# Expert results scaled by their places' weights and added to one DRAM array by accumulating scatters, in a four-layer mixer and expert kernel

## The chip, the cores and the metric

The kernel runs on one core of one Trainium2 chip. The metric is the device time in microseconds of one execution, the median of several runs. Engines are named as in the profile: PE (TensorE, with its weight loads PEld), DVE (VectorE), ACT (ScalarE), POOL (GpSimd), SP (SyncE, which here only issues transfers). "P" is 128 partitions.

## The reference

One sequence of 512 tokens with 1024 features goes through two blocks of two layers each. The first block (latent attention, retention, gated linear attention, two feed-forward networks with a convolution) is not touched. Each layer of the second block is a mixer, a layer norm, and then 16 experts in four groups, of which every token uses two:

```python
def hier_moe(x, ...):
    t = x.reshape(B * S, D)                                   # 512 x 1024
    g_prob = softmax(t @ w_group + b_group)
    g_val, g_idx = lax.top_k(g_prob, 1)
    e_logits = (einsum('td,gde->tge', t, w_expert) + b_expert)[chosen group]
    e_val, e_idx = lax.top_k(softmax(e_logits), 2)
    weights = g_val * e_val / sum(e_val)
    combine = ...                                             # 512 x 16, two entries a token
    hid = silu(t @ w_gate[e]) * (t @ w_up[e])                 # for each of 16 experts
    out = sum over e of combine[:, e] * (hid @ w_down[e])
...
ffn = hier_moe(h, ...)
h = layer_norm(DN_ALPHA * h + ffn, ln_g, ln_b)
```

## The kernel before

The kernel is one instruction stream for each engine, written in a tile framework that tracks which instruction reads and writes which tile, sets the semaphores, and puts each engine's instructions in an order of its own by priority (the order of the program) and readiness; on an engine, and on a DMA queue, they then run strictly in that order. "If" blocks are closed units: nothing moves across them.

Layers 2 and 3 (tags m0 and m1) end in the part that is changed. It has four steps:

1. `out_proj_ln` finishes the layer's first norm, one tile of 128 tokens after the other (`hN[t]`, two halves of 512 features); `store` writes each to a DRAM array `dx`. `router` computes logits on PE beside it.
2. `choose` picks two experts a token. From a running count it gives each token a `rank`, its place in the list of its expert (128 places in an expert). `places` turns this round: `eq` is a one-hot matrix of places, and 16 small matmuls give `idx`, the token of each place. `rows_of_y` computes for each token the two rows of `dy` where its results will stand, and its two weights.
3. `experts` loops over 16 experts. The weights of an expert are three transfers of 1 MB from SP into four raw buffers; each is split into a rounded half (`whi`, ACT, line 146) and a rest (`wlo`, DVE, or POOL for the third, line 147) so that three fast matmuls give one exact one. `fetch` gathers an expert's token rows from `dx` (POOL, line 1854, three buffers `X`), PE transposes them (line 1868), two products, a gate and a third product follow (lines 160 to 163), and the result `Y` (two buffers, 128 x 1024) is copied out of PSUM by ACT and DVE (lines 188 and 190) and written as a plain 512 KB transfer to `dy` (`put`, line 1859, on SP's queue among the weights). After the loop an "If" holds further rounds for experts with more than 128 tokens; it is passed over when there are none.
4. `combine` gathers for each token tile two sets of rows from `dy` (eight gathers on POOL, line 1831), scales one or both by ACT (line 1999), adds them on DVE or POOL (lines 2001 to 2006) and norms the sum (`layer_norm`, lines 1478 to 1502). After layer 2 the normed tiles go to the first projections of layer 3 (transposes at line 2057); after layer 3 they are stored as the output (line 2253).

In `combine` four of the eight gathers land in the ring of raw weight buffers (`wraw`), so that layer 3's first weights wait for them.

Of the kernel before, what the change touches and what calls it, by code (L numbers as in the profile page):

```python
# [26 lines left out]
class Ctx:  # L27
    def __init__(self, tc, ctx):
# [1631 lines left out]
NE = 16  # L1660
BIG = 1.0e30
# [11 lines left out]
def router(K, hN, A, D, tag):  # L1673

    nc, c, small = K.nc, K.const, K.small
    V, G = nc.vector, nc.gpsimd
    AD, MU, SU = ALU.add, ALU.mult, ALU.subtract
    w0, b0, gc, bcol, io, pcol, tokb, eb = (K.load(A[n]) for n in (tag + "_wr", tag + "_br", tag + "_gc", tag + "_bc", "iota", "pcol", "tokb", "eb"))  # L1680
    keep = lambda n, shape, dt=F32: K.gconst.tile(shape, dt, name=tag + n)
# [45 lines left out]
    R = dict(rank=keep("rank", [P, 8]), rhs=keep("rhs", [P, 8, 2, 16], BF16), idx=keep("idx", [P, 16], I32), row=keep("row", [P, 8], I32), eb=keep("eb", [P, 8]),  # L1727
             w=keep("w", [P, 2, 4, 1]), wr=keep("wr", [P, 8]), more=keep("more", [P, 1], I32), io=io,
             al=keep("al", [P, 1]))
    V.memset(R["al"], ALPHA)  # L1730
    rank, rhs, w12 = R["rank"], R["rhs"], R["w"]

# [9 lines left out]
    def choose():  # L1742
# [29 lines left out]
        places(K, R, K.sm(), eq_tile(K))  # L1772
# [11 lines left out]
        V.tensor_tensor(out=w12[:, 0], in0=gv, in1=m, op=MU)  # L1784
        V.tensor_tensor(out=w12[:, 1], in0=w12[:, 0], in1=r, op=MU)
# [19 lines left out]
def places(K, R, ps, eq):  # L1805
# [7 lines left out]
    V.tensor_scalar(out=R["idx"], in0=ps[:, 0:16], scalar1=OOB, scalar2=None, op0=ALU.add)  # L1813


def rows_of_y(K, R):

    V, AD, MU = K.nc.vector, ALU.add, ALU.mult
    m, f = (K.small.tile([P, 8], F32, tag=n, name=n, bufs=1) for n in ("rym", "ryf"))
    V.tensor_scalar(out=m, in0=R["rank"], scalar1=0.0, scalar2=None, op0=ALU.is_ge)  # L1820
# [4 lines left out]
    V.tensor_scalar(out=R["row"], in0=f, scalar1=OOB, scalar2=None, op0=AD)
    V.tensor_tensor(out=R["wr"], in0=R["w"].rearrange("p k t o -> p (k t o)"), in1=m, op=MU)


def gather(K, D, R, i, Y):

    K.nc.gpsimd.indirect_dma_start(out=Y, out_offset=None, in_=D["y"], in_offset=bass.IndirectOffsetOnAxis(ap=R["row"][:, i:i + 1], axis=0),  # L1831
                                   bounds_check=NE * P - 1, oob_is_err=False)


def experts(K, hN, A, D, R, rows, tag):
# [22 lines left out]
    def put(e, Y):  # L1858
        nc.sync.dma_start(D["y"][e * P:(e + 1) * P], Y)
# [72 lines left out]
    def more(e):  # L1932
# [18 lines left out]
        for i in range(2):  # L1951
# [3 lines left out]
            V.tensor_copy(out=X[:, cs], in_=ps)  # L1955
# [3 lines left out]
    with ExitStack() as ifs:  # L1959
        for rd in range(1, NR):  # L1960
            ifs.enter_context(tc.If(n > rd - 1))
            if rd == 1:
                for o in hN:
                    for x in o:
                        V.tensor_scalar(out=x, in0=x, scalar1=ALPHA, scalar2=None, op0=ALU.mult)
                V.memset(R["al"], 1.0)
            for i in range(8):
                gather(K, D, R, i, Xs[0])
                for b in range(2):
                    o = hN[i % 4][b]  # L1970
                    V.scalar_tensor_tensor(out=o, in0=Xs[0][:, b * 512:b * 512 + 512], scalar=R["wr"][:, i:i + 1], in1=o,
                                           op0=ALU.mult, op1=ALU.add)
            V.tensor_scalar(out=R["rank"], in0=R["rank"], scalar1=-float(CAP), scalar2=None, op0=ALU.add)
            rows_of_y(K, R)
            places(K, R, sm, eq)
            for e in range(NE):
                more(e)
    return Xs, gb


def combine(K, hN, D, R, Xs, gb):


    nc, V = K.nc, K.nc.vector
    AD, MU = ALU.add, ALU.mult
    Ys = Xs + [K.small.tile([P, 1024], F32, tag="Y", name="Yg")]
    for _ in range(2):
        w = K.wraw("Yw")
        Ys += [w[:, :1024], w[:, 1024:]]

    nc.scalar.activation(out=K.small.tile([P, 1], F32, tag="tab", name="tab", bufs=1), in_=R["wr"][:, 0:1], func=ACT.Sqrt)
    for i in range(8):
        gather(K, D, R, i % 2 * 4 + i // 2, Ys[i])
    for t in range(4):
        Y = Ys[2 * t:2 * t + 2]
        w = [R["wr"][:, k * 4 + t:k * 4 + t + 1] for k in range(2)]
        summed = t >= 2
        for k in range(1 + summed):
            nc.scalar.activation(out=Y[k], in_=Y[k], func=ACT.Copy, scale=w[k])  # L1999
# [298 lines left out]
```

## Time and profile before

| | us |
|---|---|
| median of three runs | 2554.08 (2550.96 to 2556.09) |
| the profiled execution | 2551.37 |
| its span in the profile | 2549.4 |
| PE busy | 2304.2 (90%) |
| DVE busy | 1503.8 (59%) |
| ACT busy | 1060.1 (42%) |
| POOL busy | 807.3 (32%) |

The span runs from the first to the last instruction that the profile shows. Engines work side by side, so busy times are not added up: what counts is which engine is the one that the others wait for in a stretch, and what ended its waits.

### The profile page before, as it was taken

To read this page: it belongs to the slowest core of one execution; us is meant where nothing else is said; L and a number is where in the kernel's file an instruction comes from. 1 tells how busy PE (TensorE), PEld (TensorE's weight loads), DVE (VectorE), ACT (ScalarE), POOL (GpSimd) and SP (SyncE) were. 2 spreads that over 40 slices of the span, in tenths; PEclk is the share of its full clock that TensorE was granted. 3 is DMA by queue.
4 is the path that set the end of the run, shared out by engine and by line. 5 is a ranking of instruction groups with operands and counts; after the bars stand their busy time and mean duration, and the time that the engine had idled before them with its cause. 6 is when DMAs were issued, how large, how long until landed. Compare 5 with 4: busy or idle time off the path is not lost. (4 is left out here: it accounts for less than half of the span.)

```text
span 2549.4 us, 32122 instructions
## 1 busy us (share of the span) xinstructions
PE 2304.2 (90%) x12404; PEld 1865.6 (73%) x12404; DVE 1503.8 (59%) x2723; ACT 1060.1 (42%) x1795; POOL 807.3 (32%) x591
## 2 busy tenths in 40 slices
PE   7999899999998999899999999996985799997882
PEld 6845558888876987777888986665874787886781
DVE  6256856525545447996564234657766645576766
ACT  4233455323334332432233233534664444445563
POOL 5321203222232322244412111216543312154534
PEclk9999999999998999999999999897997899997996
DMA  4110202233221122233342422134986322255883
GB/s 142 67 35 35 76 1 84 89 101 102 82 93 67 67 75 100 69 110 117 108 121 80 144 84 83 35 106 164 324 312 218 119 83 78 72 176 216 293 317 138
DMA packets 66633, 304.58 MB, mean 119 GB/s; under 512 B 13376, under 2 KB 14400, under 8 KB 40864
## 3 DMA queue, kind: packets, MB, share of 16 engines
q1 hardware_dynamic: 56144, 280.19, 31.5%
q0 software_dynamic: 6912, 16.79, 2.0%
q10 hardware_dynamic: 3408, 5.39, 0.7%
q8 instruction: 101, 1.65, 0.3%
q14 instruction: 68, 0.56, 0.1%
HBM read 279.13 MB, written 31.59 MB: 122 GB/s over the span
## 5 line engine op out<-in xcount | busy, mean ns | idle before, releaser
L147 POOL TENSOR_TENSOR wlo<-wraw,whi 128x683 fp32r<-128x683 f32 (+8 forms) x317 | 557.5, 1786 | 1267.1 <-ACT whi L146 1106.5
L146 ACT ACTIVATE whi<-wraw 128x683 fp32r<-128x683 f32 (+9 forms) x627 | 474.0, 817 | 384.6 <-PE mm L153 135.0
L147 DVE TENSOR_TENSOR wlo<-wraw,whi 128x683 fp32r<-128x683 f32 (+9 forms) x310 | 347.8, 1159 | 108.8 <-ACT whi L146 103.0
L152 PE MATMUL mm<-xh,whi 128*128 128x512 f32 (+2 forms) x576 | 232.1, 403 | 12.8 <-ACT xh L259 8.8
L153 PE MATMUL mm<-xl,whi 128*128 128x512 f32 (+2 forms) x576 | 228.9, 397 | 1.7 <-DVE xl L260 1.5
L154 PE MATMUL mm<-xh,wlo 128*128 128x512 f32 (+2 forms) x576 | 228.1, 396 | 0.6 <-POOL wlo L147 0.3
L152 PE MATMUL mm<-whi,xh 128*128 128x256 f32 x576 | 176.6, 307 | 13.6 <-DVE xs L508 5.0
L154 PE MATMUL mm<-whi,xl 128*128 128x256 f32 x576 | 174.7, 304 | 0.0
L153 PE MATMUL mm<-wlo,xh 128*128 128x256 f32 x576 | 172.8, 300 | 0.0
L152 PEld LDWEIGHTS mm<-xh,whi 128*128 128x128 f32 (+2 forms) x576 | 108.2, 188 | 44.8 <-ACT xh L259 9.4
L160 PE MATMUL mm<-whi,Xh 128*128 128x256 f32 x512 | 133.9, 297 | 5.0 <-ACT whi L146 5.0
L154 PE MATMUL sc<-xh,wlo 128*128 128x512 f32 x352 | 137.9, 392 | 0.0
L153 PE MATMUL sc<-xl,whi 128*128 128x512 f32 x352 | 137.5, 391 | 0.0
L152 PE MATMUL sc<-xh,whi 128*128 128x512 f32 x352 | 137.4, 390 | 0.0
L152 PEld LDWEIGHTS mm<-whi,xh 128*128 128x128 f32 x576 | 121.8, 211 | 19.0 <-issue 10.6
L161 PE MATMUL mm<-whi,Xl 128*128 128x256 f32 x512 | 130.8, 291 | 0.3
L153 PEld LDWEIGHTS mm<-xl,whi 128*128 128x128 f32 (+2 forms) x576 | 108.3, 188 | 30.8 <-DVE xl L260 4.7
L154 PEld LDWEIGHTS mm<-xh,wlo 128*128 128x128 f32 (+2 forms) x576 | 108.1, 188 | 27.8 <-POOL wlo L147 1.2
L153 PEld LDWEIGHTS mm<-wlo,xh 128*128 128x128 f32 x576 | 121.9, 212 | 0.6 <-issue 0.2
L154 PEld LDWEIGHTS mm<-whi,xl 128*128 128x128 f32 x576 | 121.6, 211 | 0.3
L160 PEld LDWEIGHTS mm<-whi,Xh 128*128 128x128 f32 x512 | 101.6, 198 | 6.8 <-ACT whi L146 6.1
L161 PEld LDWEIGHTS mm<-whi,Xl 128*128 128x128 f32 x512 | 101.4, 198 | 1.1 <-DVE Xl L257 0.9
(790 smaller groups left out, 5352.4 us busy)
## 6 DMA issues: line engine op xcount, KB each, us to landing
wraw<-in_f_up SPq DMA_DIRECT2D x44, 1024.0 KB, 4.9
wraw<-in_m_w_up SPq DMA_DIRECT2D x32, 1024.0 KB, 7.2
wraw<-in_m_w_gate SPq DMA_DIRECT2D x32, 1024.0 KB, 5.7
wraw<-in_m_w_down SPq DMA_DIRECT2D x32, 1024.0 KB, 7.2
wraw<-in_f_down SPq DMA_DIRECT2D x32, 704.0 KB, 4.1
dy<-Y SPq DMA_DIRECT2D x32, 512.0 KB, 4.4
wraw<-in_w_out SPq DMA_DIRECT2D x8, 1024.0 KB, 5.0
wraw<-in_x_out SPq DMA_DIRECT2D x8, 1024.0 KB, 4.9
```

The costliest lines, as they stand in the source:

```text
L146: nc.scalar.activation(out=hi[:, a:b], in_=raw[:, a:b], func=ACT.Copy)
L147: eng.tensor_tensor(out=lo[:, a:b], in0=raw[:, a:b], in1=hi[:, a:b].bitcast(F32), op=ALU.subtract)
L152: nc.tensor.matmul(out, ahi, bhi, start=first, stop=False)
L153: nc.tensor.matmul(out, ahi, blo, start=False, stop=False)
L154: nc.tensor.matmul(out, alo, bhi, start=False, stop=last)
L160: nc.tensor.matmul(out, a[k][0], b[k][0], start=k == 0, stop=False)
L161: nc.tensor.matmul(out, a[k][1], b[k][0], start=False, stop=False)
```

## The change

`dy` with its 2048 rows goes, and a DRAM array `dz` of 640 rows comes: 512 for the tokens and 128 for places that no token uses. `store` now also scales each half tile by ALPHA on POOL and stores it to `dz` by SP (eight instructions and eight transfers of 256 KB a layer). `choose` computes, beside `idx`, the same number clipped to a spare row (`to`), and the weight of each place (`ws`): the weights are split into three bf16 parts so that eight matmuls with `eq` give them exactly. The experts' results are scaled by `ws` where they are copied out of PSUM, always ACT for the first half and DVE for the second. `put` is an indirect transfer on POOL's queue that adds the 128 rows of `Y` to rows `to` of `dz`. `combine` loads the token tiles from `dz` by eight plain transfers of 256 KB on SP and norms them; the last step of the norm is on DVE for all four tiles. `kept` shares small tiles between the two layers. The code for further rounds is changed to match.

```diff
 def store(t):
     for i in range(2):
         nc.sync.dma_start(D["x"][t * P:(t + 1) * P, i * 512:(i + 1) * 512], hN[t][i])
+    for i in range(2):
+        z = K.u("zs")
+        G.tensor_scalar(out=z, in0=hN[t][i], scalar1=ALPHA, scalar2=None, op0=MU)
+        nc.sync.dma_start(D["z"][t * P:(t + 1) * P, i * 512:(i + 1) * 512], z)
...
-        V.tensor_tensor(out=q8, in0=flat(E), in1=eb.unsqueeze(1).to_broadcast([P, 8, 16]), op=MU)
-        V.tensor_reduce(out=R["eb"], in_=q8, axis=AX.X, op=AD)
-        rows_of_y(K, R)
+        V.tensor_copy(out=w.rearrange("p (k t) -> p k t", k=2), in_=w12)
+        for i in range(3):
+            V.tensor_copy(out=wb, in_=w)
+            V.tensor_tensor(out=R["w3"][:, :, i], in0=flat(E), in1=bc(wb, 16), op=MU)
+            if i < 2:
+                V.tensor_tensor(out=w, in0=w, in1=wb, op=SU)
+        slot_weights(K, R, pp, eq)
...
+    V.tensor_scalar(out=R["to"], in0=ps[:, 0:16], scalar1=OOB, scalar2=R["spare"], op0=ALU.add, op1=ALU.min)
+def slot_weights(K, R, ps, eq):
+    for i in range(8):
+        K.nc.tensor.matmul(ps[:, 16:64], eq[:, i], R["w3"][:, i].rearrange("p a e -> p (a e)"), start=i == 0, stop=i == 7)
+    K.nc.vector.tensor_reduce(out=R["ws"], in_=ps[:, 16:64].rearrange("p (a e) -> p e a", a=3), axis=AX.X, op=ALU.add)
...
     def put(e, Y):
-        nc.sync.dma_start(D["y"][e * P:(e + 1) * P], Y)
+        G.indirect_dma_start(out=D["z"], out_offset=bass.IndirectOffsetOnAxis(ap=R["to"][:, e:e + 1], axis=0), in_=Y, in_offset=None,
+                             bounds_check=DUMMY + P - 1, oob_is_err=True, compute_op=ALU.add)
...
-            K.copy(Y[:, cs], ps)
+            if i == 0:
+                nc.scalar.activation(out=Y[:, cs], in_=ps, func=ACT.Copy, scale=R["ws"][:, e:e + 1])
+            else:
+                V.tensor_scalar(out=Y[:, cs], in0=ps, scalar1=R["ws"][:, e:e + 1], scalar2=None, op0=ALU.mult)
...
+def combine(K, hN, D, gb):
+    nc.scalar.activation(out=K.small.tile([P, 1], F32, tag="tab", name="tab", bufs=1), in_=K.ones[:, 0:1], func=ACT.Sqrt)
     for t in range(4):
-...
         for i in range(2):
+            nc.sync.dma_start(hN[t][i], D["z"][t * P:(t + 1) * P, i * 512:(i + 1) * 512])
+    for t in range(4):
+        layer_norm(K, hN[t], *gb, last=V)
         yield t
```

## Rows read from the trace of the kernel before

**Rows 1.** Windows: start:end, length, busy us of five engines, PE clock, DMA share, GB/s.

```profile
1787.00:1940.00 153.00, 134.40 (x894) 120.56 (x893) 104.20 (x95) 97.68 (x112) 74.56 (x25) 0.93 0.86 310
...
1955.00:1983.00 28.00, 0.13 (x1) 0.13 (x2) 17.55 (x38) 11.28 (x14) 15.70 (x13) 0.53 0.54 186
1983.00:1995.00 12.00, 7.91 (x37) 6.71 (x38) 11.92 (x22) 6.93 (x13) 9.38 (x6) 0.54 0.38 137
1995.00:2020.00 25.00, 24.50 (x194) 23.07 (x194) 10.79 (x15) 8.91 (x21) 4.54 (x5) 1.00 0.29 91
...
2513.80:2549.40 35.60, 0.00 (x0) 0.00 (x0) 31.17 (x54) 12.37 (x18) 19.68 (x12) 0.50 0.40 149
```

**Rows 2.** Timeline, the end of layer 3: start, us, engine, line, tiles, [idle before].

```profile
2497.95 0.60 ACT L188 ACTIVATE Y<-sc 128x512 f32<-128x512 f32 x1 [2.00 <-PE sc L163]
...
2502.03 0.60 ACT L188 ACTIVATE Y<-sc 128x512 f32<-128x512 f32 x1 [3.21 <-issue]
...
2508.11 1.00 POOL L1831 DMA_INDIRECT m1X<-dy,m1row  x1 [16.18 <-SPq L1959]
...
2513.84 1.42 DVE L2004 SCALAR_TENSOR_TENSOR hN<-hN,m1al,m1X 128x512 f32<-128x512 f32 x2 [12.33 <-ACT m1X L1999]
...
2544.71 1.28 DVE L1502 TENSOR_TENSOR hN<-hN,lnr 128x512 f32<-128x512 f32 x2
```

**Rows 3.** Timeline, from the last expert of layer 2 to layer 3.

```profile
1953.50 0.60 ACT L188 ACTIVATE Y<-sc 128x512 f32<-128x512 f32 x1 [3.21 <-issue]
...
1959.57 1.02 POOL L1831 DMA_INDIRECT m0X<-dy,m0row  x1 [10.38 <-SPq L1959]
...
1982.87 1.11 PE L2057 MATMUL tr<-ident,hN 128*128 128x128 f32 x4 [29.45 <-POOL hN L1502]
```

**Rows 4.** Transfers between 2502.6 and 2508 (5.4 us): queue; issues, us to landing.

```profile
q1 hardware_dynamic: 144, 0.52, 24.8%
...
dy<-Y SPq DMA_DIRECT2D x1, 512.0 KB, 3.2
```

**Rows 5.** Transfers between 1959 and 1984 (25 us): POOL's queue and a gather's landing.

```profile
q0 software_dynamic: 1152, 4.19, 48.2%
...
m0X<-dy,m0row POOLq DMA_INDIRECT x3, 5.1
```

**Rows 6.** Transfers between 1787 and 1940, the experts of layer 2: issues, us to landing.

```profile
dy<-Y SPq DMA_DIRECT2D x13, 512.0 KB, 6.5
m0X<-dx,m0idx POOLq DMA_INDIRECT x10, 8.7
```

**Rows 7.** Waits of SP's queue and of PE, 1787 to 1940: us, times, longest.

```profile
SPq L1859 <- DVE Y L190: 22.8, 11, 4.1
...
PE mm L163 <- DVE wlo L147: 5.7, 5, 2.6
```

**Rows 8.** DVE's groups by form in the last stretch: busy us, mean ns, idle before.

```profile
L1478 DVE BATCH_NORM_STATS2 lnst<-hN 128x6 f32<-128x512 f32 x8 | 5.1, 675 | 0.0
...
L1502 DVE TENSOR_TENSOR hN<-hN,lnr 128x512 f32<-128x512 f32 x2 | 1.3, 678 | 0.0
...
L1484 DVE RECIPROCAL lnr<-lnr 128x1 f32<-128x1 f32 x4 | 0.6, 158 | 0.3 <-ACT lnr L1482 0.2
```

**Rows 9.** POOL's groups by form over the whole span.

```profile
L1854 POOL DMA_INDIRECT m0X<-dx,m0idx x16 | 24.0, 1498 | 52.9 <-PE tr L1868 45.9 <-DMA wraw<-in_m_w_down 5.8 <-issue 1.1
...
L582 POOL TENSOR_SCALAR D<-dp,lg 128x896 f32<-128x896 f32 x8 | 20.5, 2568 | 32.8 <-DVE At L595 32.8
```

**Rows 10.** POOL's timeline before the first fetch of layer 2.

```profile
1734.00 15.19 POOL L147 TENSOR_TENSOR wlo<-wraw,whi 128x512 fp32r<-128x512 f32 x10
1750.61 1.84 POOL L1904 MEMSET m0X<- 128x1024 f32 x2 [1.42 <-DVE hN L1502]
1758.20 1.23 POOL L1854 DMA_INDIRECT m0X<-dx,m0idx  x1 [5.75 <-DMA wraw<-in_m_w_down]
```

**Rows 11.** The same place of POOL's timeline in layer 3.

```profile
2303.18 2.01 POOL L1904 MEMSET m1X<- 128x1024 f32 x2 [10.46 <-DVE m1idx L1813]
```

More of the change, by code (lines that the diff above doesn't have):

```diff
@@ L111, in sc, with kept @@
         return self.bank("sc")
+    def kept(self, name, shape, dt=F32):
+        if name not in self.keptc:
+            self.keptc[name] = self.gconst.tile(shape, dt, name=name)
+        return self.keptc[name]
     def load(self, src, bufs=1, eng=None):
@@ L1660 @@
 NE = 16
+DUMMY = 512
 BIG = 1.0e30
@@ L1679, in router @@
     AD, MU, SU = ALU.add, ALU.mult, ALU.subtract
-    w0, b0, gc, bcol, io, pcol, tokb, eb = (K.load(A[n]) for n in (tag + "_wr", tag + "_br", tag + "_gc", tag + "_bc", "iota", "pcol", "tokb", "eb"))
-    keep = lambda n, shape, dt=F32: K.gconst.tile(shape, dt, name=tag + n)
+    w0, b0, gc, bcol, io, pcol, tokb = (K.load(A[n]) for n in (tag + "_wr", tag + "_br", tag + "_gc", tag + "_bc", "iota", "pcol", "tokb"))
+    keep = lambda n, shape, dt=F32: K.kept(n, shape, dt)
     lg = c.tile([P, 4, 20], F32, name=tag + "lg")
@@ L1726, in router @@
     flat = lambda x: x.rearrange("p a b c -> p (a b) c")
[L1727 to L1731, printed above, removed]
+    R = dict(rank=keep("rank", [P, 8]), rhs=keep("rhs", [P, 8, 2, 16], BF16), w3=keep("w3", [P, 8, 3, 16], BF16), idx=keep("idx", [P, 16], I32),
+             to=keep("to", [P, 16], I32), ws=keep("ws", [P, 16]), more=keep("more", [P, 1], I32), spare=keep("spare", [P, 1]), io=io)
+    V.tensor_scalar(out=R["spare"], in0=pcol, scalar1=float(DUMMY), scalar2=None, op0=AD)
+    rank, rhs = R["rank"], R["rhs"]
     def first_max(x, mx, oh, m):
@@ L1783, in choose @@
         V.reciprocal(out=m, in_=m)
-        V.tensor_tensor(out=w12[:, 0], in0=gv, in1=m, op=MU)
-        V.tensor_tensor(out=w12[:, 1], in0=w12[:, 0], in1=r, op=MU)
-        V.tensor_tensor(out=q8, in0=flat(E), in1=eb.unsqueeze(1).to_broadcast([P, 8, 16]), op=MU)
-        V.tensor_reduce(out=R["eb"], in_=q8, axis=AX.X, op=AD)
-        rows_of_y(K, R)
+        w12 = T3("w12", 2).rearrange("p t k -> p k t")
+        V.tensor_tensor(out=w12[:, 0], in0=gv.rearrange("p t o -> p (t o)"), in1=m.rearrange("p t o -> p (t o)"), op=MU)
+        V.tensor_tensor(out=w12[:, 1], in0=w12[:, 0], in1=r.rearrange("p t o -> p (t o)"), op=MU)
+        w, wb = (small.tile([P, 8], dt, tag="wp" + str(dt), name="wp", bufs=1) for dt in (F32, BF16))
+        V.tensor_copy(out=w.rearrange("p (k t) -> p k t", k=2), in_=w12)
[5 more added lines that the diff above has]
+        slot_weights(K, R, pp, eq)
         tot = K.sm()
@@ L1954, in more @@
                 nc.tensor.matmul(ps, h[:, k * P:k * P + P], wv[:, k, cs], start=k == 0, stop=k == 1)
-            V.tensor_copy(out=X[:, cs], in_=ps)
+            V.tensor_scalar(out=X[:, cs], in0=ps, scalar1=R["ws"][:, e:e + 1], scalar2=None, op0=ALU.mult)
         put(e, X)
@@ L1961, in experts @@
             ifs.enter_context(tc.If(n > rd - 1))
[L1962 to L1972, printed above, removed]
@@ L1973, in experts @@
             V.tensor_scalar(out=R["rank"], in0=R["rank"], scalar1=-float(CAP), scalar2=None, op0=ALU.add)
-            rows_of_y(K, R)
             places(K, R, sm, eq)
+            slot_weights(K, R, sm, eq)
             for e in range(NE):
                 more(e)
-    return Xs, gb
-def combine(K, hN, D, R, Xs, gb):
+    return gb
+def combine(K, hN, D, gb):
     nc, V = K.nc, K.nc.vector
[L1985 to L1993, printed above, removed]
-    for t in range(4):
[L1995 to L1999, printed above, removed]
-        if summed:
-            nc.gpsimd.tensor_tensor(out=Y[0], in0=Y[0], in1=Y[1], op=AD)
-        for i in range(2):
-            o, cs = hN[t][i], slice(i * 512, i * 512 + 512)
-            V.scalar_tensor_tensor(out=o, in0=o, scalar=R["al"], in1=Y[0][:, cs], op0=MU, op1=AD)
-            if not summed:
-                V.scalar_tensor_tensor(out=o, in0=Y[1][:, cs], scalar=w[1], in1=o, op0=MU, op1=AD)
-        layer_norm(K, hN[t], *gb, last=V if t == 3 else None)
@@ L2020, in prep_const @@
     ar = lambda n: np.arange(n, dtype=np.float32)
-    return dict(iota=rows(ar(P)), pcol=ar(P).reshape(P, 1), tokb=rows(np.tile(ar(4) * P - OOB, 2)), eb=rows(ar(NE) * P))
+    return dict(iota=rows(ar(P)), pcol=ar(P).reshape(P, 1), tokb=rows(np.tile(ar(4) * P - OOB, 2)))
 def layer3(K, hN, A, w_out, gb, tokens, expert_pools, route):
```

30 lines of the change are left out of this document (9 added, 21 removed).

## Prediction

> **What bounds the kernel now.** I read the page first: PE is the busiest engine, so a change to other engines counts where PE stands still. The windows show where that is. Among the experts PE works 134.4 of 153 us; then it does nothing for 28 us, works 7.91 of 12 us at a clock share of 0.54, and is full from 1995 on; after layer 3's experts it has no work at all, and DVE is busy 31.17 of the last 35.6 us [rows 1]. So each layer has two regimes: an expert stage in which PE and the transfers are both nearly full (DMA share 0.86), and a combination in which only latency and DVE count.
>
> The timelines of the two combinations come next. In layer 3 the last result is out of PSUM at 2502.63, the first gather starts at 2508.11, DVE starts at 2513.84, and its last addition ends at 2545.99, 3.4 us ahead of the span's end [rows 2]. In layer 2 the last result is ready at 1954.10 and PE gets its first normed tile at 1982.87 [rows 3]. Then the transfers [rows 4 to 6], to price the scatter, and the waits [rows 7]: among the experts PE's longest waits are for DVE's halves of the weights, not for a transfer.
>
> **The end of layer 3.** What goes: eight gathers, six wide ACT scalings, two POOL sums, twelve wide DVE sums. What comes: the wait for the last scatter, then eight plain loads. The price of one scatter alone is not in this trace. It cannot land sooner than a gather of as many rows, 5.1 us [rows 5], if the addition is free; it should not need more than that gather and then the plain write of 3.2 us [rows 4], 8.3 us. Every byte of `dz` has to be fetched and stored, with overlap; I take the middle, 6.7.
>
> All scatters write one array, so each one waits for the one before it. The 15th result is out at 2498.55 [rows 2], its scatter lands at 2505.3, and only then the 16th starts, 2.7 us after its data is ready; it lands at 2512.0. Before, the plain write landed about 2505.8 (2502.63 + 3.2), and the first gather started 2.3 us later, behind the "If"; I keep those 2.3: 2514.3. A first tile loads within 2.7 us (the 3.2 of a write of twice its size, less 0.5): 2517.0. DVE then has eight statistics (5.1 us), 16 wide steps at 0.678 (10.8) and 24 tiny ones at 0.158 (3.8): 19.7 us [rows 8], plus 1.5 in which it waits for ACT within the first tile, plus the same 3.4 for the last store. End 2541.6 against 2549.4: **-7.8 us**. With 5.1 and no wait for the 15th: 2537.3 (-12.1). With 8.3: 2544.8 (-4.6).
>
> The rule behind that wait: the Trainium skill, "DMA: Bandwidth & Descriptors", Rules for kernel authors, says that an accumulating transfer reads its destination and writes it later, that another write in between is lost, and that one must wait for the earlier one's semaphore. No accumulate is in this trace; without the wait the end would come 2.7 us sooner.
>
> **From layer 2 to layer 3.** The same chain, 548.5 us earlier: first tile loaded at 1968.5. One tile's norm is 4.9 us on DVE (a quarter of 19.7) and about 1 on ACT: PE starts near 1974.4, not 1982.87 [rows 3]. From 1983 to 1995 PE did 7.91 us at 0.54, worth 4.3 at full clock [rows 1], so it stood as if full from 1990.7, 7.8 us behind its start. The first projection's weights no longer queue behind gathers in the raw buffers, so that this lag should shrink to some 6: full from 1980.5, **-10 us**. Later tiles come every 6.3 us (4.9 and two wide splits of 0.68), about what PE needs. Bounds by the same scatter prices, with the lag kept or halved: -5 to -16. PE is the bound afterwards (24.50 of 25 us), so this reaches the end.
>
> **Ahead of the experts.** Eight scalings of 128 x 512 on POOL; by its scaling of 128 x 896 in 2.57 us [rows 9] 1.47 each, 11.8 us a layer. In layer 2 POOL splits weights for 15.2 us until 1749.2 and then, around its memsets, stands idle 1.4 and 5.75 us before the first fetch at 1758.20 [rows 10]. The last tile's two scalings fit there; the earlier six (8.8 us) push the splits. If all splits stay ahead of the fetch, it is late by 11.8 - 7.2 = 4.6 us; if some move behind it, by nothing. In layer 3 POOL idles 10.46 us [rows 11]: about nothing. The eight stores share SP's queue with the next tile's rows of `dx`: late scalings delay those too. DVE loses nine small instructions and gains about as many; eight small matmuls run while PE waits for the fetch. I take **+3 us** for both layers, 0 to +9.
>
> **In the expert stage.** Evictions keep their engines and lengths. `put` leaves SP, where it held the queue 22.8 us in 11 waits for DVE's half of the result [rows 7], and goes to POOL, where a gather of rows takes 1.5 us of instruction [rows 9]: 13 x 1.5 = 20 us on 74.56 of 153 [rows 1]. Behind a waiting `put` stand a fetch and a third weight's rest. The fetch fills one of three buffers well ahead. The rest is used an expert later; PE hardly waits for POOL today. I cost that order at nothing; its cover is this slack of one expert.
>
> The transfers are the dear part. A plain put takes 24.8% of 5.4 us of all DMA engines, 1.34 us; a gather 48.2% of 25 us over eight, 1.51 us [rows 4, 5]. A scatter that adds lies between 1.34 (fetching is free) and 2.85 (both in turn); nearest is the sum, since the bytes are the sum's. So 13 x 1.51 = 19.6 us come on top of 0.86 x 153 = 131.6: 151 of 153 us. It fits with no slack. At a share of 0.95 the stretch would take 159 us, +6; if the share stays at 0.86, 176 us, +23; against it SP's loads start sooner, worth up to -3 if one in seven of the 22.8 us counts. I take **+4 us a layer, +8**, as no engine waits long for transfers now.
>
> The Trainium skill speaks against the change here: "Collectives: The Full Stack", The bandwidth ceiling, says that a reducing transfer reads two sources over one ring and so runs at half a copy's rate. By it a scatter takes 2.68 us instead of 1.34, an added 17.4 us in the stretch, close to the sum of the two rows; if the row's 1.34 held, the stage would cost nothing and the change comes to -15.
>
> **The sum.** -7.8 - 10 + 3 + 8 = -6.8 us. The profiled execution took 2551.37 (span 2549.4): 2544.6. The three runs' median is 2.7 above it, so I forecast a median of 2547, in a range of its own of 2541 to 2553.
>
> **Rivals.**
> *The stage swallows the extra fetching.* PE waits 5.7 us for DVE and nothing like it for a transfer [rows 7], and SP loses its waits. Then the stage costs 0 to -2 a layer and the total is -15 to -19: 2535 to 2539.
> *DMA becomes the bound of the stage* (the other side). For it: 151 of 153 us, and landings that are already long, 6.5 us for a write that takes 3.2 alone and 8.7 for a fetch [rows 4, 6]. Against it: the share is not yet a wait. At +15 a layer (a share of 0.90) the total is -18 + 3 + 30 = +15: 2569. It decides from +7.5 a layer, where the gain is gone, and is slower than 0.2% from +10.
> *Scatters in a chain.* Each waits for the one before. From the first fetch to the last result are 196 us [rows 3, 10], 12.2 an expert; if a loaded scatter takes more than 10.7 beside 1.5 us of POOL, the chain sets the pace. At 12 us, a fetch's 8.7 and a plain write's 3.2: 16 x 13.5 = 216, +20 a layer, 2579. Against it: 8.7 is for rows that do not gate anything.
> *The gain is lost ahead of the experts and at the joins.* If the fetches come late by 4.6 in both layers and the "If" waits for POOL's queue longer than 2.3, the two combinations give -10 and the rest takes it: -10 + 9 + 4 = +3: 2556.
>
> **Chances.** Forecast 0.34, swallowed 0.25, DMA the bound 0.22, lost ahead 0.11, chain 0.08. One measurement here tells 0.2% (5.1 us) from nothing. The forecast's own range lies two thirds below -5 us (0.22 faster, 0.12 same); swallowed is faster; lost ahead splits 0.06 same and 0.05 slower; the other two are slower. Faster 0.47, same 0.18, slower 0.35. The range leaves out the chain and the worst of the bound stage above, and the best corner (both lower bounds, -28) below: 2528 to 2576.
>
> **What would show it.** PE's first transpose of layer 3 some 20 us behind the last eviction, not 28.8; the span's end some 40 us behind layer 3's last eviction, not 46.8. The DMA share among the experts near 0.95, with the stage (first to last matmul) 0 to 6 us longer; PE or ACT waiting for weight transfers would show the bound stage; POOL's puts starting late behind the landing of the one before would show the chain. The first fetch of layer 2 at most 5 us later than today, of layer 3 not later. It is wrong if a scatter lands in over 10 us, or if its share of DMA time is far from 2.85 us.

## The result, and the profile after

| | before | after |
|---|---|---|
| median, us | 2552.52 (2548.41 to 2556.09) | 2582.87 (2581.32 to 2590.0) |
| ratio | | 1.0125 [1.01, 1.015] |
| profiled execution, its span | 2551.37, 2549.4 | 2582.56, 2580.8 |

The change makes the kernel 30 us slower; the forecast was 7 us faster. Below, a "landing" is the time from a transfer's issue to its end as the profile gives it, and a "result" is `Y`, an expert's output as it leaves PSUM ("evicted"). Both profiles, cut at the same six events, show where (us; "stage" is from PE's first transpose of the experts' tokens to the last result out of PSUM):

| stretch | before | after | difference | forecast |
|---|---|---|---|---|
| start to layer 2's experts | 1762.81 | 1773.66 | +10.9 | +3 |
| stage of layer 2 | 191.3 | 208.3 | +17.0 | +4 |
| last result to layer 3's first transpose | 28.8 | 29.7 | +1.0 | -8.5 (-10 with the lag behind it) |
| layer 3 to its experts | 326.6 | 328.9 | +2.3 | (within the +3) |
| stage of layer 3 | 193.1 | 198.7 | +5.6 | +4 |
| last result to the end | 46.8 | 41.5 | -5.2 | -7.8 |

**Ahead of layer 2's experts.** POOL's timeline, the place of [rows 10] (start, duration, what ended the idle time before):

```profile
1745.36 9.18 POOL L153 TENSOR_TENSOR wlo<-wraw,whi 128x512 fp32r<-128x512 f32 x6
1754.51 7.85 POOL L1733 TENSOR_SCALAR zs<-hN 128x512 f32<-128x512 f32 x5
1762.31 1.86 POOL L1916 MEMSET m0X<- 128x1024 f32 x2
1766.61 1.26 POOL L1862 DMA_INDIRECT m0X<-dx,idx  x1 [2.44 <-issue]
```

Five of the eight scalings stand in one piece behind six splits, and the memset and the first fetch behind them: 1766.61 where it was 1758.20. The fetch also needs `idx` from DVE, and that came 4.9 us later too (before, then after):

```profile
1757.14 0.17 DVE L1813 TENSOR_SCALAR m0idx<-sm 128x16 int32<-128x16 f32 x1
```

```profile
1762.03 0.17 DVE L1832 TENSOR_SCALAR idx<-sm 128x16 int32<-128x16 f32 x1
```

DVE's small steps from the last logits to `idx` took 10.1 us beside the scalings (from 1752.12) and 6.9 before (from 1750.41).

**Among layer 2's experts.** The waits between 1780 and 1985 (us, times, longest), then the transfers between 1798 and 1958, to be held against [rows 6, 7], and the window, against [rows 1]:

```profile
ACT Y L1909 <- DMA dz<-Y,to: 18.8, 6, 6.3
...
POOL dz L1867 <- DVE Y L1911: 16.4, 2, 11.1
POOL dz L1867 <- ACT Y L1909: 14.7, 3, 9.3
DVE Y L1911 <- DMA dz<-Y,to: 12.2, 5, 4.8
```

```profile
q0 software_dynamic: 3024, 8.34, 24.8%
...
dz<-Y,to POOLq DMA_INDIRECT x12, 11.9
m0X<-dx,idx POOLq DMA_INDIRECT x10, 9.5
```

```profile
1798.00:1958.00 160.00, 136.48 (x894) 122.78 (x894) 112.33 (x95) 98.75 (x112) 103.65 (x37) 0.93 0.91 290
1983.00:2012.00 29.00, 0.30 (x2) 0.33 (x3) 9.47 (x37) 4.38 (x9) 3.45 (x5) 0.50 0.57 146
```

New among the long waits is the eviction itself: ACT and DVE stand 31.0 us in eleven waits because the buffer that they would fill still belongs to a scatter. There are two result buffers; each is taken until its scatter has landed, 11.9 us (the median) after its issue, and that scatter starts only when the one before it into `dz` has landed. Behind the waiting eviction, in ACT's and DVE's order, stand splits that PE needs. One place of ACT's and PE's timelines, where `eh` is the rounded half of the next expert's gated product:

```profile
1918.00 0.69 ACT L1909 ACTIVATE Y<-sc,ws 128x512 f32<-128x512 f32 x1 [6.28 <-DMA dz<-Y,to]
1918.59 0.38 ACT L262 ACTIVATE eh<-tr 128x256 fp32r<-128x256 f32 x1
```

```profile
1919.02 0.50 PE L166 MATMUL sc<-whi,eh 128*128 128x512 f32 x1 [3.10 <-ACT eh L262]
```

The DMA share is 0.91, not 0.95.

**The joins.** Timelines of POOL, SP, DVE and PE behind layer 2's last result (out at 1981.95), answering [rows 3]:

```profile
1982.01 2.16 POOL L1867 DMA_INDIRECT dz<-Y,to  x1 [5.29 <-DVE Y L1911]
1992.06 1.55 POOL L1867 DMA_INDIRECT dz<-Y,to  x1 [7.89 <-DMA dz<-Y,to]
```

```profile
1998.98 3.70 SPq L1989 DMA_DIRECT2D hN<-dz  x8
```

```profile
2001.55 0.69 DVE L1484 BATCH_NORM_STATS2 lnst<-hN 128x6 f32<-128x512 f32 x1 [1.32 <-DMA hN<-dz]
```

```profile
2011.70 1.51 PE L2041 MATMUL tr<-ident,hN 128*128 128x128 f32 x6 [33.26 <-DVE lnr L1490]
```

The fifteenth scatter is issued when the sixteenth result is already there; the sixteenth waits for it until 1992.06 and lands after 6.0 us; the loads start at 1998.98, behind the "If". After layer 3 the same, with the wait ended by the transfer each time (answers to [rows 2]):

```profile
2539.05 1.56 POOL L1867 DMA_INDIRECT dz<-Y,to  x1 [6.07 <-DMA dz<-Y,to]
2546.54 1.56 POOL L1867 DMA_INDIRECT dz<-Y,to  x1 [5.93 <-DMA dz<-Y,to]
```

```profile
2554.86 3.65 SPq L1989 DMA_DIRECT2D hN<-dz  x8
```

The landings of the two sixteenth scatters, from the transfers of 1990 to 2000 and of 2545.8 to 2556:

```profile
dz<-Y,to POOLq DMA_INDIRECT x1, 6.0
```

```profile
dz<-Y,to POOLq DMA_INDIRECT x1, 6.7
```

### The profile page after: what moved, and what is told of

It is laid out like the page before. It is cut to its first block, busy times and chain, and to the rows that moved or that the text cites. A ratio compares the mean times of both kernels' runs of the same rounds, so it can differ in the third digit from the quotient of the medians.

```text
span 2580.8 us, 32154 instructions
## 1 busy us (share of the span) xinstructions
PE 2314.2 (90%) x12420; PEld 1871.0 (72%) x12420; DVE 1504.3 (58%) x2715; ACT 1053.9 (41%) x1785; POOL 860.5 (33%) x607
## 5 line engine op out<-in xcount | busy, mean ns | idle before, releaser
L153 POOL TENSOR_TENSOR wlo<-wraw,whi 128x683 fp32r<-128x683 f32 (+8 forms) x317 | 564.0, 1811 | 1231.0 <-ACT whi L152 1118.7
L153 DVE TENSOR_TENSOR wlo<-wraw,whi 128x683 fp32r<-128x683 f32 (+9 forms) x310 | 364.0, 1211 | 126.5 <-ACT whi L152 122.0
L166 PE MATMUL mm<-whi,Xh 128*128 128x256 f32 x512 | 139.7, 305 | 4.3 <-ACT whi L152 4.3
L167 PE MATMUL mm<-whi,Xl 128*128 128x256 f32 x512 | 136.5, 299 | 0.2 <-DVE Xl L263 0.2
L158 PEld LDWEIGHTS mm<-whi,xh 128*128 128x128 f32 x576 | 121.0, 210 | 19.4 <-issue 10.7
```

The source lines that it names most:

```text
L153: eng.tensor_tensor(out=lo[:, a:b], in0=raw[:, a:b], in1=hi[:, a:b].bitcast(F32), op=ALU.subtract)
L158: nc.tensor.matmul(out, ahi, bhi, start=first, stop=False)
L166: nc.tensor.matmul(out, a[k][0], b[k][0], start=k == 0, stop=False)
L167: nc.tensor.matmul(out, a[k][1], b[k][0], start=False, stop=False)
```

## The experiments

All times below are medians with the interval of their ratio to the kernel before, which ran beside each of them (2551.1 to 2552.5). The stretches are those of the table above, each from one profiled execution. Executions of the kernel before alone spread from 2544 to 2558 us, so a difference of under some 4 us in a stretch is not read.

| run | median | ratio | to layer 2's experts | stage 2 | gap | stage 3 | tail |
|---|---|---|---|---|---|---|---|
| e1_skip_spare | 2573.9 | 1.0081 [1.0061, 1.0102] | 1779.5 | 202.6 | 25.9 | 200.2 | 38.4 |
| e2_y3 | 2571.5 | 1.008 [1.006, 1.0101] | 1775.5 | 191.4 | 32.8 | 199.9 | 41.5 |
| e3_no_add | 3091.6 | 1.2112 [1.2089, 1.2134] | 1773.5 | 192.2 | | | |
| e4_plain_put | 2521.6 | 0.9879 [0.9857, 0.9902] | 1777.3 | 195.7 | 1.4 | 204.8 | 7.1 |
| e5_fold | 2567.0 | 1.0057 [1.0035, 1.008] | 1764.8 | 206.5 | 29.8 | 203.8 | 39.9 |
| e6_two_arrays | 2561.8 | 1.0042 [1.0024, 1.006] | 1765.2 | 195.6 | 28.8 | 204.1 | 39.9 |
| e7_two_y3_skip | 2563.7 | 1.0042 [1.0029, 1.0055] | 1765.7 | 194.0 | 27.6 | 203.3 | 38.4 |
| e8_fold_y3_skip | 2551.4 | 1.0001 [0.9989, 1.0013] | 1766.4 | 193.4 | 32.3 | 197.2 | 37.4 |
| e9_late_put | 2551.7 | 0.9999 [0.9989, 1.0009] | 1764.5 | 191.7 | 33.2 | 198.3 | 37.8 |
| e10_last_scatter_only | 2530.1 | 0.9908 [0.9891, 0.9924] | 1766.3 | 190.5 | 24.3 | 190.6 | 33.9 |
| e11_fold_y3 | 2557.8 | 1.002 [1.001, 1.003] | 1768.6 | 190.8 | 33.4 | 199.9 | 38.6 |
| e12_norm_order | 2558.8 | 1.0024 [1.0014, 1.0034] | 1765.7 | 190.7 | 32.1 | 193.8 | 45.3 |
| e13_own_arrays | 2531.1 | 0.9928 [0.991, 0.9946] | 1764.7 | 191.2 | 25.0 | 189.2 | 33.8 |
| e14_mixed | 2552.0 | 0.9998 [0.9984, 1.0012] | 1772.2 | 195.0 | 28.5 | 196.0 | 37.8 |
| e15_own_add | 2546.5 | 0.9982 [0.9972, 0.9991] | 1768.3 | 193.8 | 23.8 | 199.7 | 34.0 |
| e16_chain_no_add | 2523.2 | 0.9889 [0.9873, 0.9906] | 1767.0 | 184.1 | 25.0 | 191.2 | 34.0 |
| e17_chain_add | 2544.6 | 0.9969 [0.9953, 0.9984] | 1765.7 | 191.9 | 29.1 | 197.8 | 34.9 |

The theories: **A**, the scatters' bytes; **B**, the result buffers that are held until a scatter lands; **C**, the chain of scatters into one array; later **D**, the scalings on POOL; **E** and **F**, the scatters' place and time on POOL.

**e1_skip_spare**

```diff
-ap=R["to"][:, e:e + 1] ... bounds_check=DUMMY + P - 1, oob_is_err=True
+ap=R["idx"][:, e:e + 1] ... bounds_check=511, oob_is_err=False
```

> Places without a token are left out of the scatter (their index is out of bounds and not an error) instead of being added to spare rows, so about half of the 128 rows of each scatter move; the result is the same. Theory A (the transfers of the expert stage are full, bytes cost): half of the added bytes go, the stages (first transpose to last eviction, 208 and 199 us after the change, 191 and 193 before) shorten by about 10 and 3, total -13 to -20. Theory B (a result buffer is held until its scatter has landed, and ACT and DVE stand behind it): landing falls from 11.9 to perhaps 8 us, stages shorten by 10 to 15 and the two scatters at each end land 2 us sooner each, total -20 to -30. Theory C (each scatter waits for the one before): as B at the ends, little in the stages, total -8 to -10.

POOL's queue falls from 24.8% to 15.8% of the DMA engines' time, the landing among layer 2's experts only from 11.9 to 11.3 us, and ACT and DVE still wait 22.6 us for result buffers. The 9 us that it gives are shared by stage, gap and tail. The total is what C expected, but not its place: layer 2's stage gives 5.7 us and starts 5.8 later in this execution. Half the bytes are worth something, but the held buffers stay: A alone falls.

**e2_y3**

```diff
-Y = small.tile([P, 1024], F32, tag="Y", name="Y")
+Y = small.tile([P, 1024], F32, tag="Y", name="Y", bufs=3)
...
-K.phase(tag, units=14)
+K.phase(tag, units=13)
```

> Three result buffers instead of two, paid for with one of 14 general buffers of the stage. Theory B: the waits of ACT and DVE for landed scatters (31 us in layer 2's stage) nearly go, stages 208 and 199 fall by 10 to 15 and 3 to 5, total -13 to -20. Theory A: no change, within 3 us. Theory C: no change in the stages either, since the scatters still go one at a time.

```profile
POOL dz L1867 <- DMA dz<-Y,to: 22.9, 4, 9.0
...
ACT Y L1909 <- DMA dz<-Y,to: 5.2, 2, 2.7
...
DVE Y L1911 <- DMA dz<-Y,to: 1.8, 1, 1.8
```

These are the waits between 1780 and 1985 again. With all the bytes and the whole chain, layer 2's stage is back at 191.4 us: its 17 us are the held buffers, B. (The median landing fell too, to 7.8 us; e11 shows the same gain without that.) Now POOL waits for the chain, where little stands behind it. What the stage gains is partly given back in the gap (32.8): the scatters now lag behind the results. Layer 3's stage does not move, and the total gains 11.4 us, less than B's 13 to 20.

**e3_no_add** (no addition: later results overwrite earlier ones, so the output lacks sums)

```diff
-bounds_check=DUMMY + P - 1, oob_is_err=True, compute_op=ALU.add)
+bounds_check=DUMMY + P - 1, oob_is_err=True)
```

> The same indirect scatter of 128 rows without the addition (rows of dz are overwritten, the sums are left out). Theory A: the fetching of the destination goes, DMA busy time of POOL's queue halves, stages fall to 191 to 196. Theory B: landing falls from 11.9 to 7 or 8 us, stages fall by 10 to 15. If neither (the indirect form itself is dear): landing stays above 10 us and the stages at 200 or more.

The total can't be compared: with other sums layer 3's tokens crowd some experts, and the "If"'s further rounds run. Layer 2's stage can: 192.2 us with two buffers and the chain kept. POOL's queue takes 15.1% and a scatter lands in 9.6 us, not 11.9. In e1 the queue took as little with the addition (15.8%), a scatter landed in 11.3 us and the stage stayed at 202.6. So the buffers hold the engines because the addition makes each link of the chain long.

**e4_plain_put** (results go by plain transfers to an array that nobody reads; the sums are left out)

```diff
-G.indirect_dma_start(out=D["z"], out_offset=..., compute_op=ALU.add)
+nc.sync.dma_start(D["y"][e * P:(e + 1) * P], Y)
```

> The result goes to the old array dy by a plain transfer on SP, as before the change; the sums are left out of dz, everything else of the change stays. Theories A, B and C: stages as before, 191 to 194; the ends shorten further, since no scatter has to land before the tiles load: 29.8 and 41.5 us (last eviction to the first transpose of layer 3, and to the end) fall to about 18 and 32. What stays over the kernel before is then what the scalings and stores ahead of the experts cost, about 10 us in layer 2. Total -30 to -45 against the changed kernel.

61 us below the change. But the loads of `dz` then wait for no expert, and the norms run inside the stages, which is why the gap is 1.4 us; this is a floor and prices nothing by itself. e10 mends that.

**e5_fold** (also the base of all that follow)

```diff
-z = K.u("zs")
-G.tensor_scalar(out=z, in0=hN[t][i], scalar1=ALPHA, scalar2=None, op0=MU)
-nc.sync.dma_start(D["z"][...], z)
+nc.sync.dma_start(D["z"][...], hN[t][i])
...
-V.tensor_tensor(out=w12[:, 0], in0=gv..., in1=m..., op=MU)
+V.scalar_tensor_tensor(out=w12[:, 0], in0=gv..., scalar=1 / ALPHA, in1=m..., op0=MU, op1=MU)
...
-layer_norm(K, hN[t], *gb, last=V)
+layer_norm(K, hN[t], *gb, last=V, eps=1e-5 * (1 / ALPHA) ** 2)
```

> The change's kernel without the eight scalings of 128 x 512 on POOL ahead of the experts: the plain tile is stored, the places' weights are divided by ALPHA and the norm's epsilon by its square, so that the normed rows are the same. Theory D (the scalings on POOL, and DVE's small steps slowed beside them, hold the first fetch): the first transpose of layer 2's experts comes 8 to 11 us sooner, near 1764, and the time falls from 2582.9 to 2572 to 2575. Rival (the extra stores and the weights' loads in the queues hold the fetch, whoever scales): 0 to 3 us sooner, 2579 to 2583.

```profile
1751.00 1.84 POOL L1914 MEMSET m0X<- 128x1024 f32 x2 [1.41 <-DVE hN L1508]
1758.62 1.27 POOL L1860 DMA_INDIRECT m0X<-dx,idx  x1 [5.78 <-DVE wp L1801]
```

POOL's timeline at the place of [rows 10]: the fetch starts at 1758.62, as before the change, and PE at 1764.8, 8.9 us sooner than with the scalings. DVE's steps from the last logits to `idx` are back at 6.9 us. The stores to `dz` are still there and cost nothing that shows: D holds, its rival falls. The median gains 15.9 us, more than those 8.9; ahead of layer 3's experts it is 4.1 (328.9 to 324.8), at the limit of what is read, and the rest stands in no single stretch that one execution could tell.

**e6_two_arrays**, **e7_two_y3_skip**, **e8_fold_y3_skip**

```diff
-G.indirect_dma_start(out=D["z"], ...
+G.indirect_dma_start(out=D["z2" if e % 2 else "z"], ...
...
+nc.sync.dma_start(D["z2"][t * P:(t + 1) * P, i * 512:(i + 1) * 512], hN[t][i])
...
+nc.sync.dma_start(z2[t][i], D["z2"][t * P:(t + 1) * P, i * 512:(i + 1) * 512])
...
+V.tensor_tensor(out=hN[t][i], in0=hN[t][i], in1=z2[t][i], op=ALU.add)
```

e6 is e5 with these lines (the weights' factor is then 2 / ALPHA), e7 adds the edits of e1 and e2 to it, e8 is e5 with the edits of e1 and e2 and without these lines.

> As e5_fold, but even experts add into one array and odd ones into a second, both begun from the plain tile; the combination loads both and adds them on DVE (eight more additions of 128 x 512, some 0.7 us each, and eight more loads). Theory C (a scatter waits for the one before it into the same array, and the two result buffers stay taken meanwhile): the landing falls from 9.9 us to some 6 to 7, layer 2's expert stage from 208 us to 190 to 195, the gap from its last eviction to layer 3's first transpose from 29.8 to 22 to 25 us; the tail gains some 7 us by the earlier landing and loses some 7 by the additions. Total 2550 to 2558. Rival (the landing is long because the queues are full, not because of the one before): landing above 9 us, stage as in e5_fold, total as e5_fold or some 5 us longer.

> As e6_two_arrays, with three result buffers (and one buffer fewer of the shared ones), and unused places skipped, so that a scatter carries half the rows. Theories B and C together: no eviction waits for a scatter; both expert stages as before (191 to 194 us), gap 18 to 22 us, 2542 to 2552. If what is left of the loss is the scatters' place on POOL's queue, layer 3's stage stays near 199 and the time at 2552 to 2558.

> As e7 but with one array: three result buffers, unused places skipped, no scalings on POOL. Beside e7 it prices the chain once buffers don't hold the engines: by theory C the gap after layer 2's experts stays at 26 to 30 us and the tail at 38 to 40, total 2556 to 2562. If the chain costs nothing by itself, as e7 plus or minus 3.

e6: with two buffers and no immediate predecessor, layer 2's stage is 195.6 us, and no eviction waits for a transfer there. So the buffers are held by the chain times the landing, and either a third buffer or a second array frees them. The gap hardly falls: the second array brings eight loads and eight additions of its own. e8 is the best of the three, and at 2551.4 equal to the kernel before: scalings, held buffers and unused places are together worth 31.5 us, the whole loss. It came 4.6 us below what was expected; e6 came 4 and e7 12 us above, with some 204 us in layer 3's stage where e8 has 197. Why the second array costs there, and no longer in layer 2, was not found. The scatters of e8 after layer 2's last result (1959.80), POOL and SP:

```profile
1959.01 1.56 POOL L1865 DMA_INDIRECT dz<-Y,idx  x1 [3.53 <-issue]
...
1966.01 1.55 POOL L1865 DMA_INDIRECT dz<-Y,idx  x1 [3.78 <-DMA dz<-Y,idx]
1972.75 1.54 POOL L1865 DMA_INDIRECT dz<-Y,idx  x1 [5.20 <-DMA dz<-Y,idx]
```

```profile
1979.88 3.65 SPq L1987 DMA_DIRECT2D hN<-dz  x8
```

Three scatters of half the rows follow each other at 7.0 and 6.7 us, and the loads come 7.1 us behind the third. The last one landed in 6.2 us, and in 4.9 after layer 3, where full ones took 6.0 and 6.7: a lone scatter's time falls far less than its bytes.

**e9_late_put**

```diff
             fetch(e + 2)
+        if e > 1:
+            put(e - 2, Ys[e - 2])
...
-    down(e - 1, hs, Wd)
+    Ys.append(down(e - 1, hs, Wd))
```

> As e8_fold_y3_skip, but each scatter stands one expert later in POOL's order, behind the next expert's fetch and weights. Theory E (a scatter that waits for its result or for the scatter before it holds the fetches and the thirds of weights behind it on POOL, and this is what is left of layer 3's stage: 197 us in e8, 193 before): layer 3's stage falls to 193 to 195 and the first eviction gaps of experts 1 to 3 to those of before (10.1, 14.7, 8.2); the joins may grow by up to a landing where two scatters are left at the end; total 2546 to 2553. Rival (POOL's order is free, the stage's rest is DVE's and ACT's scaled evictions): stage unchanged within 2 us, total 2551 to 2560.

No change, and the times between the first four experts' results in layer 3 stay (12.6, 16.6, 9.8 us; 12.6, 16.4, 9.8 in e8). E falls: the order that the prediction had costed at nothing costs nothing.

**e10_last_scatter_only** (fifteen of sixteen sums are left out, in this and in e13, e15, e16 and e17)

```diff
 def put(e, Y):
+    if e < NE - 1:
+        nc.sync.dma_start(D["y"][e * P:(e + 1) * P], Y)
+        return
```

> As e8_fold_y3_skip, but only the sixteenth expert's result is scattered; the fifteen others are written by plain transfers on SP's queue into an array that nobody reads, so that their sums are left out of the output. The join then holds one scatter without a predecessor. Theory C: the gap from the last eviction to layer 3's first transpose falls from 32.3 by the two landings of the chain (13 to 14 us) to 18 to 20 us, the tail from 37.4 to 29 to 31 us; total 2528 to 2536 with both stages within 3 us of those of before. Rival (the join is long because of the loads and the norm behind the scatter): the gap stays above 26 us, total above 2542.

21 us below e8: 2.9 and 6.6 in the stages, 8.0 in the gap, 3.5 in the tail. The gap stays above what C expected (18 to 20): the single scatter landed only after 9.9 us there, against 6.0 after layer 3. A 1 MB load runs beside it in layer 2; that this is the reason is not shown.

**e11_fold_y3** is e8 without e1's edit.

> As e8_fold_y3_skip without the skipping: every scatter carries its 512 KB again. If bytes bind once no buffer does (theory A): the stages grow by 5 to 10 us each, total 2562 to 2575. By theories B and C bytes count only through the landing: both stages within 3 us of e8's, gap and tail longer by 1 to 3 us each, total 2553 to 2559.

6.4 us above e8, with both stages within 3 us of it: bytes don't bind the stages, as B and C said. Beside e5 it is also the cleanest test of B: the third buffer alone takes layer 2's stage from 206.5 to 190.8 us, with a median landing of 11.2 and 10.9 us, and the evictions' waits for scatters fall from 27.0 to 9.4.

**e12_norm_order**

```diff
-st = small.tile([P, 2, 6], F32, tag="lnst", name="lnst")
+st = small.tile([P, 2, 6], F32, tag="lnst", name="lnst", bufs=1)
...
-mv = small.tile([P, 2], F32, tag="lnmv", name="lnmv")
+mv = small.tile([P, 2], F32, tag="lnmv", name="lnmv", bufs=1)
```

> As e8_fold_y3_skip, but the norm's statistics have one small buffer in place of two, so that DVE cannot take the statistics of later tiles ahead of the first tile's scaling. In e8 DVE has its first statistic at 1982.5 and PE its first tile at 1992.1, 9.7 us, where the prediction took 5.9. If DVE's order makes the difference: 7 to 8 us in place of 9.7 in the gap, 2548 to 2551. Rival (what the statistics wait for are the loads and ACT's steps between): no change, 2551 to 2554.

Slower by 7.4 us, with a tail of 45.3 for 37.4; the gap is the same. The statistics of later tiles fill DVE while it would wait for the first tile's loads and ACT's steps; they are not what delays the first tile.

**e13_own_arrays**, **e15_own_add**, **e16_chain_no_add**, **e17_chain_add**: a square.

```diff
 def put(e, Y):
     if e < NE - 1:
-        nc.sync.dma_start(D["y"][e * P:(e + 1) * P], Y)
+        G.indirect_dma_start(out=D[tag + str(e)], out_offset=...idx..., bounds_check=511, oob_is_err=False)
         return
```

e15 adds `compute_op=ALU.add` to it, e16 sends all fifteen to one array, `D["m00"]`, and e17 does both.

> As e10_last_scatter_only (only the sixteenth expert's result is added to the output's array), but the fifteen others go by scatters from POOL without addition, each into an array of its own that nobody reads, so that no scatter waits for another. Theory F (a scatter costs by being issued on POOL: some 1.6 us each in which DVE's subtractions from SBUF are slowed): DVE's 22 subtractions of 128 x 2048 in layer 3's stage take 3.2 to 3.4 us as in e8, not 2.9 as in e10; layer 3's stage comes to 195 to 199 us where e10 has 190.6; the joins stay as in e10 (24 and 34 us); total 2533 to 2540. Theory C alone (what e8 loses against e10 is all the chain): subtractions at 2.9 us, stage 190 to 192, total within 3 us of e10's 2530.

> One of a square of four with e13_own_arrays (no chain, no addition, 2531): here the fifteen unread scatters add, each into an array of its own, so that there is addition and no chain; only the sixteenth result reaches the output's array. If the addition's traffic costs time in the stages: 2538 to 2546, with layer 3's stage at 194 to 197 us. If the chain is what costs (theory C): within 4 us of 2531, layer 3's stage 189 to 192.

> The fifteen unread scatters go without addition into one array, so that there is a chain and no addition; only the sixteenth result reaches the output's array. By theory C: POOL waits 10 to 20 us a stage for the scatter before, layer 3's stage 194 to 197 us, total 2538 to 2546. If the chain costs in the joins alone, where it is not kept here: within 4 us of 2531.

> Both: the fifteen unread scatters add into one array, so that the stages are those of e8_fold_y3_skip, and only the sixteenth scatter, into the output's array, is without a predecessor. Against e8 (2551) it prices the chain at the joins: by theory C the two joins give back 7 and 4 us, total 2538 to 2542. If the stages' part of the chain is small, 2531 to 2537.

| median, us | an array each | one array |
|---|---|---|
| no addition | 2531.1 | 2523.2 |
| addition | 2546.5 | 2544.6 |

Two theories fall here. F: e13 issues its scatters from POOL as e8 does and takes no longer than e10, which issues none. And C, for the stages: with three buffers one array costs nothing, with or without addition. What costs is the addition: 15.3 us with an array each, 21.4 with one. The chain costs where nothing hides it: e8, where the last scatter has a predecessor in its own array, is 6.8 us slower than e17. That is not the whole price of the chain at the joins, since e17 still waits for a chain in layer 2: its fifteenth scatter was issued behind the sixteenth, had to wait for the fourteenth, and the "If" waited for its landing, 4.6 us after that of the sixteenth (e17's timeline of POOL):

```profile
1960.85 1.99 POOL L1869 DMA_INDIRECT dz<-Y,idx  x1 [0.17 <-issue]
1963.63 1.54 POOL L1866 DMA_INDIRECT dym<-Y,idx  x1 [0.80 <-DMA dym<-Y,idx]
1973.94 0.15 POOL L2022 MEMSET mv<- 128x32 f32 x1 [8.76 <-DMA dym<-Y,idx]
```

Why one array without addition (e16) is 7.9 us faster than fifteen (e13), with 7 us of it in layer 2's stage, was not taken apart. The rows of layer 3's stage, by form (busy us, mean ns), of e16 and e17:

```profile
L153 DVE TENSOR_TENSOR wlo<-wraw,whi 128x2048 fp32r<-128x2048 f32 x22 | 68.4, 3109 | 19.4 <-ACT whi L152 19.4
...
L1866 POOL DMA_INDIRECT dym<-Y,idx x15 | 21.5, 1432 | 29.7 <-ACT whi L152 11.4 <-DVE el L263 7.1 <-issue 5.6
```

```profile
L153 DVE TENSOR_TENSOR wlo<-wraw,whi 128x2048 fp32r<-128x2048 f32 x22 | 72.9, 3312 | 22.0 <-ACT whi L152 21.9
...
L1866 POOL DMA_INDIRECT dym<-Y,idx x15 | 29.7, 1981 | 36.5 <-DMA dym<-Y,idx 13.9 <-DVE Xl L263 6.2 <-ACTq L1973 5.3
```

Then PE's waits for DVE's subtractions in the same stretch of e16 and e17 (us, times, longest), the largest in e17 and the one that grows:

```profile
PE mm L169 <- DVE wlo L153: 5.2, 5, 2.8
```

```profile
PE mm L169 <- DVE wlo L153: 10.1, 6, 4.6
```

And POOL's queue between 1798 and 1950:

```profile
q0 software_dynamic: 3145, 5.81, 10.3%
```

```profile
q0 software_dynamic: 3048, 5.60, 16.2%
```

With the addition POOL's instruction takes 0.55 us more, DVE's subtraction beside it 0.2 us more, and the queue 16.2% in place of 10.3% for as many bytes. Layer 3's stage is 6.6 us longer with it (10.5 from e13 to e15), and PE's waits for those subtractions grow by 4.9 (from 7.7 to 15.2 in e13 and e15): there the addition reaches the path. Whether it makes DVE late through POOL's longer instruction or through the weights' transfers was not taken apart and stays open.

**e14_mixed** has e6's second array in layer 2 alone, on e8.

> As e8_fold_y3_skip, with the second array of e7_two_y3_skip in layer 2 alone (odd experts add there; both arrays are loaded and added on DVE), one array in layer 3. By theory C the gap between the layers falls from e8's 32.3 us to e7's 27.6 us and the rest stays: 2545 to 2549, 0.1 to 0.3% below before. Rival (the order of the engines in layer 3's stage moves more than the chain gives): layer 3's stage away from e8's 197 us by over 4 us, total 2551 to 2558.

The gap falls to 28.5 us as C said, but the time does not: 2552.0 (2544.8 to 2556.6). The profiled execution was the slowest of its ten. No version here beats the kernel before and keeps the sums.

## Why the prediction was wrong

The range ended at 2576, the time is 2583. From the forecast to the profiled execution are 38 us: 13 in the stage of layer 2, 11 in the gap between the layers, 10 ahead of the experts, and 4 in the tail and layer 3's stage. By its own steps:

- **The expert stage: this step failed.** "Evictions keep their engines and lengths" had the engines right, and the lengths nearly so (688 and 744 ns among layer 2's experts, 597 and 691 before), and left out what an eviction must wait for. The text named what stands behind a waiting `put` on POOL, and not what stands behind the buffer that it keeps. Before, a buffer came free when a plain write landed, with no predecessor; now two links of the chain lie in between. That is 17 us of layer 2's 208.3 (e2, e11, e6, e3), where the sum had 4. In layer 3 the evictions waited 19.6 us in all and a third buffer brought nothing; what remains there is the addition (square).
- **The DMA price was right.** 12 scatters and 10 fetches take 24.8% of 160 us, 39.7 us; e10's nine fetches take 4.2% of 152, so 0.71 each; a scatter takes (39.7 - 7.1) / 12 = 2.7 us against 2.85 forecast. The Trainium skill's half rate ("Collectives: The Full Stack", The bandwidth ceiling), which the page states of a ring's reduction and not of this kind of transfer, gave an estimate of 2.68, and this case agrees. So does the square: 10.3% and 16.2% less 4.2% for the fetches is 6.1 against 12.0%, twice the time with the addition. And the forecast that a fuller DMA alone would not set the pace held too: e11 has 26.5% on that queue and a stage of 190.8.
- **Ahead of the experts** the price was too low: 4.6 us at worst in layer 2, 8.9 measured (e5). The eight scalings took 13.3 us, not 11.8, and of the 7.2 us of idle time in [rows 10], which the sum took as room for them, POOL still stood idle for 2.4 in front of the fetch: 4.6 + 1.5 + 2.4 = 8.5, for a fetch that came 8.4 later. The sum also left DVE out: `idx`, which the fetch reads, was ready only 0.9 us before the fetch (at 1757.31), and DVE's steps to it took 3.2 us longer beside the scalings.
- **The gap.** Forecast 20.3 us from last result to first transpose, measured 29.7. The wait for the fifteenth scatter was 10.1 instead of 2.7, since that scatter itself had only then been issued: the chain ran late out of the stage. The landing was 6.0 (6.7 forecast), the "If" and first load 3.5 instead of 5.0, the first tile's norm 10.1 instead of 5.9. That last figure of the forecast counted DVE's work and 1 us of ACT; the later loads and ACT's steps lie between them (e12).
- **The tail.** Gain 5.2, forecast 7.8: the sixteenth scatter was issued 7.2 us after its data, not 2.7. It landed in 6.7, as forecast, and the loads started 1.6 later (2.3 forecast). From DVE's first statistic to its last step are 19.7 us (2557.41 to 2577.1), 17.05 of them busy; the forecast had 19.7 busy and 1.5 of waiting.
- **The rivals.** "Scatters in a chain", with a chance of 0.08 and 2579, came nearest: its 20 us in layer 2 are the 17 measured, by another way (through the result buffers, not POOL's pace) and in one layer only, so that its total is near by luck. "DMA becomes the bound" gave 2569 for a reason that e11 excludes. One of the prediction's own signs of being wrong did come: a landing of over 10 us, 11.9 among the experts.

## What to carry to other kernels

When a write out of a buffer becomes slower or is made to wait for another write, ask first who fills that buffer next: count buffers against landings, including the wait for the predecessor, and name what stands behind the filler on its engine. A chain of scatters into one array is free only where nobody waits for the landing (the addition itself cost 15 to 21 us here, with or without a chain); at a stage's end its last links lie bare on the path, some 7 us each in e8's rows, and e10, without them, gave back 8.0 and 3.5 us at the two ends. And small work put on an engine ahead of a join is paid for if that engine's order lets it stand in front of what the join waits for, or if it slows the engine that computes it; here a change of constants made the work needless.

## What the hardware showed that was not expected

- An accumulating scatter alone landed in 6.0 and 6.7 us for 512 KB (the change) and in 6.2 and 4.9 us for the used half of it (e8); among layer 2's experts the medians were 7.8 us (e2) to 11.9 (the change) for full ones and 8.4 (e8) to 12.1 (e15) for half ones. The next link of a chain was issued 0.7 to 0.8 us after a landing.
- DVE's subtractions of 128 x 2048, with both inputs in SBUF, took 2.90 us in layer 3's stage of e10 and 3.38 in e8, where POOL also issues the scatters; DVE's scalings out of PSUM took 0.746 and 0.745 (groups by form of that stage, e10, then e8; busy us, mean ns). The Trainium skill, "SBUF — State Buffer", Who interferes with whom, says that a DVE instruction with two SBUF inputs contends with a GpSimd instruction that reads SBUF, and that one with at most one, outside the two-port modes, does not contend; in these rows the first grew and the second did not. That it is the issuing of the scatters that reads there is not shown.

```profile
L153 DVE TENSOR_TENSOR wlo<-wraw,whi 128x2048 fp32r<-128x2048 f32 x22 | 63.7, 2899 | 17.9 <-ACT whi L152 17.9
...
L1912 DVE TENSOR_SCALAR Y<-sc,ws 128x512 f32<-128x512 f32 x16 | 11.9, 746 | 18.9 <-PE sc L169 18.9
```

```profile
L153 DVE TENSOR_TENSOR wlo<-wraw,whi 128x2048 fp32r<-128x2048 f32 x22 | 74.4, 3381 | 19.7 <-ACT whi L152 19.6
...
L1909 DVE TENSOR_SCALAR Y<-sc,ws 128x512 f32<-128x512 f32 x16 | 11.9, 745 | 14.1 <-PE sc L169 14.1
```

- In e13 such a lengthening did not set the time: it has 3.15 us there and the same total as e10. Whether the 3.3 to 3.5 us of e17 and e15 did is the question left open above.
- Scatters into one array ran no slower than into fifteen (median landings among layer 2's experts of 8.8 and 10.6 us without addition, 10.7 and 12.1 with it), and POOL's instruction was shorter with one: 1.43 us against 1.94 without addition, 1.98 against 2.38 with it.
